# A hybrid decoder block on one core: gating and its loads on GpSimd, a staged gate table, and 512-wide products with u

## The chip, the cores and the metric

One core of a Trainium2 chip runs the whole program. TensorE (PE) multiplies, VectorE (DVE) and ScalarE (ACT) work on tiles and read PSUM, GpSimd (POOL) works on tiles in SBUF and issues indirect DMAs, SyncE (SP) issues the other DMAs. The metric is the device time of one execution in microseconds; a verdict rests on several runs.

## The reference

The block is `out = norm(h + PEER(norm(h)))` with `h = x + [attention, rwkv] @ W_out`, for 256 tokens of width 2048. The change lies in the last part, PEER: for each token and each of 8 heads two score lists of 128 keys are cut to their best 16, the 256 sums of pairs again to the best 16, and these name 16 of 128 x 128 = 16384 experts, with a softmax gate each.

```python
    hpre = jnp.einsum('cd,chkd->chk', xc, u[ec])
    act = jax.nn.gelu(hpre, approximate=False) * gc
    return jnp.einsum('chk,chkd->cd', act, v[ec])
```

All of it is float32, and the kernel keeps that precision by splitting operands into a high and a low part of type fp32r.

## The kernel before

It doesn't gather rows of u. It multiplies all 16384 rows of u with all 256 tokens, applies Gelu, multiplies with a dense table of gates (zero where an expert isn't chosen), and then goes through the rows of v in use only. The stages concerned, in time order:

*Hidden products* (`hidden`): 128 keys i2, each with the 128 experts (., i2). For a key `gemm` makes 16 steps of three 256-wide products: high weights with high tokens, high weights with low tokens, low weights with high tokens (lines 218 to 220). The weights come in halves of 512 KB on SP's queue (L197), split by ACT (L204) and DVE (L205). A Gelu (L1106) writes the key's 128x256 result into a tile A of eight keys.

*Beside them*, three generators get shares of a budget for every quarter of a key (`beside`, `run`): `both_choices` finds the experts, `tables` builds the table of gates, `scatter` writes rows away. Their `yield` values are costs against that budget; they set only where an instruction stands in its engine's order. Engines work in that order and wait by semaphores.

*The table* (`table`): for four columns (tokens) at a time DVE marks first and second key numbers (L931, L930), POOL scales the second mark by the gate's high part (L936), ACT by its low part (L938); TensorE multiplies the marks (L954), ACT and DVE bring the two halves of the result into a tile gc (L982, L983). Every 16 columns the tile goes to DRAM (`gate_d`), and POOL adds up (L969 to L976) which experts are in use. `places` then gives each expert a row in DRAM (`rows_d`).

*Rows* (`scatter`): for keys 0 to 125, DVE multiplies a key's Gelu results by its gates (L1074) and copies the expert's number beside them (L1088); POOL writes the 128 rows of 257 values to their places by an indirect DMA (L1089). The gates come back from `gate_d` in 16 loads of 1 MB (L1059, on SP's queue), one per eight keys.

*Products with v*: the last two keys skip the detour. Their gated results are split and multiplied with v as soon as the pool of the earlier stages is closed. For the others, blocks of 128 rows are read back once all scatters have landed, the rows of v are gathered (L1172, POOL), split and multiplied (L1159 to L1161), 108 blocks in all. A last norm follows.

The tiles A, gt (gates), at (rows), ob, gc, and later those of v all come from one pool of 16 buffers, so that a new one waits for the last reader of an old one.

Of the kernel before, what the change touches and what calls it, by code (L numbers as in the profile page):

```python
# [10 lines left out]
F32 = mybir.dt.float32  # L11
# [10 lines left out]
P = 128  # L22
# [132 lines left out]
def block_kernel(ctx: ExitStack, tc: tile.TileContext, x, cols, consts, w_lora, w_gate, w_rkv, w_qkv,  # L155
# [631 lines left out]
    nc.sync.dma_start(iota, consts[:, K_IO:K_IO + P])  # L787
    nh = mp.tile([P, KT, S], F32R, tag="mh", name="nh")
    nl = mp.tile([P, KT, S], F32R, tag="ml", name="nl")
    nhk, nlk = (lambda kt: nh[:, kt, 0:T]), (lambda kt: nl[:, kt, 0:T])  # L790
    sck = [chunked(f"sc{t}", 16, NKEY) for t in range(2)]

    def scores(b, ps):
# [5 lines left out]
        nc.vector.tensor_tensor(xn, hg(b), rstd2, op=ALU.mult)  # L799
        split(nh[:, b, :], nl[:, b, :], xn)  # L800
        yield
# [51 lines left out]
    def choose(t):  # L853
# [53 lines left out]
        yield 0.3  # L907
        nc.scalar.activation(tr, pt, AF.Copy)
        chosen[t] = tr
        yield 0.1  # L910

# [3 lines left out]
    def table(t):  # L915


        while t not in chosen:
            yield 0
        tr = chosen[t]  # L920
        b3 = [P, NB, P]
        col = lambda i, n: tr[:, i, n:n + NB].unsqueeze(2).to_broadcast(b3)
        row = iota.unsqueeze(1).to_broadcast(b3)
        made = {}

        def marks(n):
# [7 lines left out]
        def weighted(n):  # L934
            o1, o2, og = made[n]
            nc.gpsimd.tensor_tensor(og[:, :, 0, :], o2, col(2, n), op=ALU.mult)  # L936
            for i in range(NB):
                nc.scalar.activation(og[:, i, 1, :], o2[:, i, :], AF.Copy, scale=tr[:, 3, n + i:n + i + 1])  # L938

        marks(0)  # L940
        yield 0.1
        for q in range(8):
            gc = big(f"gc{q % 2}").rearrange("p (e t) -> p e t", t=16)
            late = []
            for n in range(q * 16, q * 16 + 16, NB):
                if n + NB < P:
                    marks(n + NB)
                weighted(n)
                yield 1.4
                o1, _, og = made.pop(n)  # L950
                for i in range(0, NB, 2):
                    ps = bank(("ch", "pw", "ch", "px")[(n // 2 + i // 2) % 4], [P, 2, 2, P])
                    for j in range(2):
                        nc.tensor.matmul(ps[:, j].rearrange("p a b -> p (a b)"), o1[:, i + j, :],  # L954
                                         og[:, i + j].rearrange("p a b -> p (a b)"), start=True, stop=True,
                                         skip_group_check=True)
                    late.append((ps, n + i - q * 16))
                    yield 0
                    if len(late) > 1:
                        ps_, k = late.pop(0)  # L960
                        evict(gc, ps_, k)
                        yield 0.45
            while late:
                evict(gc, *late.pop(0))
                yield 0.45
            nc.sync.dma_start(gate_d[:, t * 8 + q, :], gc.rearrange("p e t -> p (e t)"))

            w = big("mt")[:, 0:1024].rearrange("p (e t) -> p e t", t=8)
# [11 lines left out]
    def evict(gc, ps, k):  # L980
        g = gc[:, :, k:k + 2].rearrange("p e t -> p t e")
        nc.scalar.activation(g, ps[:, :, 1, :], AF.Copy)  # L982
        nc.vector.tensor_tensor(g, g, ps[:, :, 0, :], op=ALU.add)  # L983
# [124 lines left out]

# [181 lines left out]
```

## Time and profile before

| | |
|---|---|
| median of 3 runs | 2053.21 us (2050.47 to 2059.78) |
| profiled execution, its own time | 2050.37 us |
| its span, first to last instruction | 2048.6 us |
| TensorE, DVE, ACT, POOL busy | 94%, 72%, 51%, 32% of the span |
| mean granted clock of TensorE | 0.979 of full speed |

Busy shares are means over stages with different limits; what a stage waits for is read from its waits and windows. Times are in us from the span's start unless marked ns. A line number is the line of the kernel's source that issued the instruction; some lines are helpers with many callers.

### The profile page before, as it was taken

To read this page: it belongs to the slowest core of one execution; us is meant where nothing else is said; L and a number is where in the kernel's file an instruction comes from. 1 tells how busy PE (TensorE), PEld (TensorE's weight loads), DVE (VectorE), ACT (ScalarE), POOL (GpSimd) and SP (SyncE) were. 2 spreads that over 40 slices of the span, in tenths; PEclk is the share of its full clock that TensorE was granted. 3 is DMA by queue.
4 is the path that set the end of the run, shared out by engine and by line. 5 is a ranking of instruction groups with operands and counts; after the bars stand their busy time and mean duration, and the time that the engine had idled before them with its cause. 6 is when DMAs were issued, how large, how long until landed. Compare 5 with 4: busy or idle time off the path is not lost. (4 is left out here: it accounts for less than half of the span.)

```text
span 2048.6 us, 35160 instructions
## 1 busy us (share of the span) xinstructions
PE 1929.4 (94%) x13598; PEld 1810.1 (88%) x13598; DVE 1482.4 (72%) x2343; ACT 1054.0 (51%) x1636; POOL 654.5 (32%) x558
## 2 busy tenths in 40 slices
PE   7898999999999999998999999999993999999996
PEld 7798999999889999998999999999992888888885
DVE  6676878766557888999898887765553666666666
ACT  4544454454455444466676666534441655555554
POOL 7211221100000000135654545455547433333332
PEclk9999999999999999999999999999996999999998
DMA  8999322224665555455565655699898977888784
GB/s 251 259 255 243 100 78 93 88 84 154 211 218 188 185 178 176 164 172 185 197 217 188 215 182 180 229 306 297 286 296 273 368 275 278 299 286 299 280 292 149
DMA packets 163976, 444.14 MB, mean 217 GB/s; under 512 B 14368, under 2 KB 85024, under 8 KB 147168
## 3 DMA queue, kind: packets, MB, share of 16 engines
q1 hardware_dynamic: 140016, 306.02, 48.0%
q0 software_dynamic: 23792, 135.87, 18.1%
q8 instruction: 107, 1.75, 0.3%
q14 instruction: 61, 0.50, 0.1%
HBM read 380.07 MB, written 61.76 MB: 216 GB/s over the span
## 5 line engine op out<-in xcount | busy, mean ns | idle before, releaser
L204 ACT ACTIVATE whi<-raw 128x1024 fp32r<-128x1024 f32 (+1 forms) x408 | 431.2, 1057 | 501.9 <-PE ps_gm L219 220.9
L205 DVE TENSOR_TENSOR wlo<-raw,whi 128x1024 fp32r<-128x1024 f32 (+1 forms) x408 | 530.4, 1303 | 213.9 <-ACT whi L204 212.3
L220 PE MATMUL ps_gm<-nh,wlo 128*128 128x256 f32 x2048 | 585.6, 286 | 22.4 <-DVE wlo L205 21.7
L218 PE MATMUL ps_gm<-nh,whi 128*128 128x256 f32 x2048 | 583.0, 285 | 0.0
L219 PE MATMUL ps_gm<-nl,whi 128*128 128x256 f32 x2048 | 582.5, 284 | 0.0
L220 PEld LDWEIGHTS ps_gm<-nh,wlo 128*128 128x128 f32 x2048 | 396.1, 193 | 27.3 <-DVE wlo L205 26.9
L218 PEld LDWEIGHTS ps_gm<-nh,whi 128*128 128x128 f32 x2048 | 396.4, 194 | 0.0
L219 PEld LDWEIGHTS ps_gm<-nl,whi 128*128 128x128 f32 x2048 | 396.2, 193 | 0.0
L236 DVE TENSOR_TENSOR vlo<-vraw,vhi 128x2048 fp32r<-128x2048 f32 x108 | 247.8, 2296 | 146.3 <-ACT vhi L235 140.8
L235 ACT ACTIVATE vhi<-vraw 128x2048 fp32r<-128x2048 f32 x108 | 205.9, 1913 | 151.6 <-DVE vlo L236 144.4
L1172 POOL DMA_INDIRECT vraw<-in_v_dram,ag x108 | 145.0, 1343 | 285.0 <-PE ps_gm L1161 213.0
L218 PE MATMUL ps_gm<-xh,whi 128*128 128x256 f32 x640 | 192.8, 301 | 1.1 <-ACT whi L204 1.1
L220 PE MATMUL ps_gm<-xh,wlo 128*128 128x256 f32 x640 | 185.4, 290 | 1.3 <-DVE wlo L205 1.2
L219 PE MATMUL ps_gm<-xl,whi 128*128 128x256 f32 x640 | 186.0, 291 | 0.0
L1089 POOL DMA_INDIRECT rows_d<-at,place x126 | 143.3, 1137 | 117.4 <-DVE at L1088 66.4
L936 POOL TENSOR_TENSOR ob<-ob,pick 128x512 fp32r<-128x512 f32 x64 | 107.0, 1677 | 187.8 <-DVE ob L930 180.2
L220 PEld LDWEIGHTS ps_gm<-xh,wlo 128*128 128x128 f32 x640 | 123.1, 192 | 2.5 <-DVE wlo L205 1.9
L218 PEld LDWEIGHTS ps_gm<-xh,whi 128*128 128x128 f32 x640 | 123.3, 193 | 2.0 <-ACT whi L204 1.3
L219 PEld LDWEIGHTS ps_gm<-xl,whi 128*128 128x128 f32 x640 | 123.4, 193 | 0.7
L938 ACT ACTIVATE ob<-ob,pick 128x128 fp32r<-128x128 f32 x256 | 83.7, 389 | 61.4 <-DVE ob L930 61.3
L969 POOL TENSOR_TENSOR mt<-gc 128x1024 f32<-128x1024 f32 x16 | 55.0, 3434 | 166.3 <-DVE gc L983 166.3
L795 POOL DMA_DIRECT2D skb<-in_sk_dram x16 | 8.6, 539 | 250.7 <-ACT mh L235 167.7
(1528 smaller groups left out, 4027.2 us busy)
## 6 DMA issues: line engine op xcount, KB each, us to landing
raw<-in_u_dram SPq DMA_DIRECT2D x256, 512.0 KB, 4.1
raw<-in_w_rkv_dram SPq DMA_DIRECT2D x48, 512.0 KB, 6.9
raw<-in_w_qkv_dram SPq DMA_DIRECT2D x48, 512.0 KB, 3.3
rows_d<-zt SPq DMA_DIRECT2D x23, 1028.0 KB, 13.8
raw<-in_w_out_dram SPq DMA_DIRECT2D x32, 512.0 KB, 3.4
raw<-in_wq_dram SPq DMA_DIRECT2D x32, 512.0 KB, 3.4
gate_d<-gc SPq DMA_DIRECT2D x16, 1024.0 KB, 6.2
gt<-gate_d SPq DMA_DIRECT2D x16, 1024.0 KB, 9.0
```

The source lines that it names most:

```text
L204: nc.scalar.activation(hi[:, :n], raw[:, :n], AF.Copy)
L205: state["dve"] = nc.vector.tensor_tensor(lo[:, :n], raw[:, :n], hi[:, :n].bitcast(F32), op=ALU.subtract)
L218: nc.tensor.matmul(ps, a, xh(kt), start=first and k == 0, stop=False)
L219: nc.tensor.matmul(ps, a, xl(kt), start=False, stop=False)
L220: state["mm"] = nc.tensor.matmul(ps, b, xh(kt), start=False, stop=last and k == HK - 1)
L235: nc.scalar.activation(hi, src, AF.Copy)
L236: nc.vector.tensor_tensor(lo, src, hi.bitcast(F32), op=ALU.subtract)
L936: nc.gpsimd.tensor_tensor(og[:, :, 0, :], o2, col(2, n), op=ALU.mult)
L938: nc.scalar.activation(og[:, i, 1, :], o2[:, i, :], AF.Copy, scale=tr[:, 3, n + i:n + i + 1])
L969: nc.gpsimd.tensor_tensor(w, gc[:, :, 0:8], gc[:, :, 8:16], op=ALU.add)
L1089: s_ = nc.gpsimd.indirect_dma_start(out=rows_d, out_offset=bass.IndirectOffsetOnAxis(ap=place[:, i2:i2 + 1], axis=0), in_=at, in_offset=None)
L1172: nc.gpsimd.indirect_dma_start(out=raw, out_offset=None, in_=vf, in_offset=bass.IndirectOffsetOnAxis(ap=ag[:, T:ROW].bitcast(I32), axis=0))
```

## The change

Five things change together.

1. The tokens' high and low parts lie side by side, and `gemm_wide` multiplies the high weights with both in one 512-wide product, then the low weights with the high part in a 256-wide one. ACT copies the second half out, DVE adds the first, and the Gelu is issued a step into the next key.
2. The multiplication by the gates (`gated`) and the copy of the experts' numbers (now for seven keys at once) go to POOL, for the 126 scattered keys. The loads of gates go to POOL's queue.
3. The table is staged: marks, scaled marks and products of a group of columns stand in three successive turns. DVE makes the second mark and its gate in one operation per column; ACT scales that by the ratio of low and high part, worked out once in `choose`. POOL's multiplication L936 is gone.
4. The tile gc holds blocks of eight keys together, so that evictions write runs of eight.
5. `place` moves to a pool that stays open. The table's share of the budget is 0.43 for 0.45, a scatter's cost 1.5 for 2.35.

```diff
+    def gemm_wide(ps, xk):
+
...
+                nc.tensor.matmul(ps.rearrange("p z t -> p (z t)"), hi[:, k * P:(k + 1) * P],
+                                 x_.rearrange("p z t -> p (z t)"), start=i + k == 0, stop=False, skip_group_check=True)
+                state["mm"] = nc.tensor.matmul(ps[:, 0, :], lo[:, k * P:(k + 1) * P], x_[:, 0, :], start=False,
+                                               stop=i == 1 and k == HK - 1, skip_group_check=True)
...
-            o1, o2 = (ob[:, i * NB * P:(i + 1) * NB * P].rearrange("p (n k) -> p n k", n=NB) for i in range(2))
-            og = ob[:, 2 * NB * P:].rearrange("p (n z k) -> p n z k", n=NB, z=2)
-            nc.vector.tensor_tensor(o2, row, col(1, n), op=ALU.is_equal)
+            o1 = ob[:, 0:NB * P].rearrange("p (n k) -> p n k", n=NB)
+            og = ob[:, NB * P:3 * NB * P].rearrange("p (n z k) -> p n z k", n=NB, z=2)
             nc.vector.tensor_tensor(o1, row, col(0, n), op=ALU.is_equal)
-            made[n] = o1, o2.bitcast(F32), og
...
+        def weighted(n, i):
+            og = made[n][1]
+            c_ = lambda k: tr[:, k, n + i:n + i + 1]
+            nc.vector.tensor_scalar(og[:, i, 0, :], iota, c_(1), c_(2), op0=ALU.is_equal, op1=ALU.mult)
+            nc.scalar.activation(og[:, i, 1, :], og[:, i, 0, :].bitcast(F32), AF.Copy, scale=c_(3))
...
+        for n in range(0, P + 2 * NB, NB):
+            pairs = [half_in() for _ in range(1)] if late else []
+            if n < P:
+                marks(n)
+                yield 0.7
+            if pairs:
+                other_in(pairs.pop())
+                pairs.append(half_in())
+                yield 0.45
+            if NB <= n <= P:
+                for i in range(2):
+                    weighted(n - NB, i)
+                    yield 0.25
+            if pairs:
+                other_in(pairs.pop())
+                yield 0.45
+            if NB <= n <= P:
+                for i in range(2, NB):
+                    weighted(n - NB, i)
+                    yield 0.25
+            if 2 * NB <= n:
+                for i in range(0, NB, 2):
+                    product(n - 2 * NB, i)
+                made.pop(n - 2 * NB)
+                yield 0.02
+        while late:
+            other_in(half_in())
+            yield 0.45
         chosen[t, "table"] = True
...
-    place = sp.tile([P, P], I32, name="place")
+    place = cp.tile([P, P], I32, name="place")
...
-            nc.sync.dma_start(gts[g], gate_d[:, :, g * P:(g + 1) * P])
+            nc.gpsimd.dma_start(gts[g], gate_d[:, :, g * P:(g + 1) * P])
...
-    def gated(i2):
+    def gated(i2, eng=nc.gpsimd):
 
         if i2 % 7 == 0:
             rows[0] = big("at")
+            n = min(7, NKEY - i2)
+            eng.tensor_copy(rows[0][:, 0:n * ROW].rearrange("p (n c) -> p n c", c=ROW)[:, :, T].bitcast(I32),
+                                  eint[:, i2:i2 + n])
         g = gates_of(i2 // 8)
         if i2 % 8 == 1:
             gates_of(i2 // 8 + 1)
             gts.pop(i2 // 8 - 1, None)
         at = rows[0][:, i2 % 7 * ROW:(i2 % 7 + 1) * ROW]
         k = i2 % 8
-        nc.vector.tensor_tensor(at[:, 0:T].rearrange("p (q t) -> p q t", q=KT),
-                                As[i2 // 8][:, k, :].rearrange("p (q t) -> p q t", q=KT),
-                                g[:, :, 16 * k:16 * k + 16], op=ALU.mult)
+        eng.tensor_tensor(at[:, 0:T].rearrange("p (q t) -> p q t", q=KT),
+                          As[i2 // 8][:, k, :].rearrange("p (q t) -> p q t", q=KT),
+                          g.rearrange("p q (t b) -> p q t b", b=8)[:, :, :, k], op=ALU.mult)
...
-            nc.vector.tensor_copy(at[:, T:ROW].bitcast(I32), eint[:, i2:i2 + 1])
...
-            yield 2.35
-
+            yield 1.5
...
-            ps = bank("gm")
-            yield from gemm(ps[:, :T], P, nhk, nlk)
-            state["gelu"] = nc.scalar.activation(As[-1][:, i2 % 8, 0:T], ps[:, :T], AF.Gelu)
-            hid["n"] = i2 + 1
+            ps = bank("gm", [P, 2, S])
+            wide = gemm_wide(ps, nk)
+            next(wide)
+            if summed:
+                gelu()
+            yield
+            yield from wide
+            part = small("part")
+            nc.scalar.activation(part, ps[:, 1, :], AF.Copy)
+            nc.vector.tensor_tensor(part, part, ps[:, 0, :], op=ALU.add)
+            summed.append((part, As[-1][:, i2 % 8, :], i2))
+        gelu()
...
-    beside = [[both_choices(), 0.55, 0.0], [tables(), 0.45, 0.0], [scatter(), 1.0, 0.0]]
+    beside = [[both_choices(), 0.55, 0.0], [tables(), 0.43, 0.0], [scatter(), 1.0, 0.0]]
...
-            ah, al_ = halves_of(gated(i2)[:, 0:T])
+            ah, al_ = halves_of(gated(i2, nc.vector)[:, 0:T])
```

POOL's order, where the scatters begin, before: `at` is a tile of seven rows, and what stands in brackets is whose semaphores the instruction waits for (DMASW0 to 7 are those of POOL's own DMAs, used in turn).

```order
L973 TENSOR_TENSOR mt<-mt 128x128 [waits Pool_49]
L974 TENSOR_TENSOR act_8194<-act_8194,mt 128x128 [waits Pool_49]
L1089 DMA rows_d<-at,place 39936x257 [waits DVE_49]
L1089 DMA rows_d<-at,place 39936x257 x5
L1089 DMA rows_d<-at,place 39936x257 [waits DMASW6_49]
L1089 DMA rows_d<-at,place 39936x257 [waits DMASW7_49,DVE_49]
L1089 DMA rows_d<-at,place 39936x257 [waits DMASW0_49,DVE_49]
L1089 DMA rows_d<-at,place 39936x257 [waits DMASW1_49,DVE_49]
```

And of the change, some way into the same stretch (`A` a tile of eight keys, `gt` its gates):

```order
L1122 TENSOR_TENSOR at<-A_9660,gt_14731 128x256
L1122 TENSOR_TENSOR at<-A_10268,gt_14863 128x256 [waits DMASW5_49]
L1136 DMA rows_d<-at,place 39936x257 [waits DMASW4_49,Pool_49]
L1136 DMA rows_d<-at,place 39936x257 [waits Pool_49]
L1104 DMA gt_14981<-gate_d 128x16x128 [waits DMASW6_49]
L1122 TENSOR_TENSOR at<-A_10268,gt_14863 128x256 x2
L1136 DMA rows_d<-at,place 39936x257 [waits DMASW7_49,Pool_49]
L1136 DMA rows_d<-at,place 39936x257 [waits DMASW0_49,Pool_49]
L1114 COPY at<-eint 128x7
L1122 TENSOR_TENSOR at<-A_10268,gt_14863 128x256
L1122 TENSOR_TENSOR at<-A_10268,gt_14863 128x256 [waits Pool_49]
L1136 DMA rows_d<-at,place 39936x257 [waits DMASW1_49,Pool_49]
```

Before, POOL has nothing but scatters there, each waiting for DVE. Now a multiplication stands for each, mostly in pairs ahead of a pair of scatters, with the loads and copies between them, and the waits are for POOL itself.

DVE's order in the table stage, before (L205 is the split of weights, L983 the eviction):

```order
L930 TENSOR_TENSOR ob<-iota,pick 128x512
L931 TENSOR_TENSOR ob<-iota,pick 128x512
L205 TENSOR_TENSOR wlo<-raw,whi 128x1024 x2
L983 TENSOR_TENSOR gc_12201<-gc_12201,ps_ch 128x2x128
L930 TENSOR_TENSOR ob<-iota,pick 128x512
L931 TENSOR_TENSOR ob<-iota,pick 128x512
L930 TENSOR_TENSOR ob<-iota,pick 128x512
L205 TENSOR_TENSOR wlo<-raw,whi 128x1024
L983 TENSOR_TENSOR gc_12201<-gc_12201,ps_pw 128x2x128
L931 TENSOR_TENSOR ob<-iota,pick 128x512
```

And of the change (L954 the scaled marks, L1167 the addition that follows a wide product, L996 the eviction):

```order
L205 TENSOR_TENSOR wlo<-raw,whi 128x1024
L954 TENSOR_SCALAR ob<-iota,pick 128x128 x4
L948 TENSOR_TENSOR ob<-iota,pick 128x512
L205 TENSOR_TENSOR wlo<-raw,whi 128x1024
L1167 TENSOR_TENSOR part<-part,ps_gm 128x256
L996 TENSOR_TENSOR gc_11420<-gc_11420,ps_ch 128x2x16x8
L996 TENSOR_TENSOR gc_11420<-gc_11420,ps_pw 128x2x16x8
L954 TENSOR_SCALAR ob<-iota,pick 128x128 x3
L205 TENSOR_TENSOR wlo<-raw,whi 128x1024
L954 TENSOR_SCALAR ob<-iota,pick 128x128 x5
L205 TENSOR_TENSOR wlo<-raw,whi 128x1024
```

One of two 512-wide marks is gone, four 128-wide ones stand in its place, and each key adds a 256-wide addition.

ACT's order of the change, where the Gelu (L1151) of key 104 opens a new tile A:

```order
L204 ACTIVATE whi<-raw 128x1024 [waits DMAHW1_49,PE_49,Activation_49]
L204 ACTIVATE whi<-raw 128x1024 [waits DMAHW2_49,PE_49,Activation_49]
L1166 ACTIVATE part<-ps_gm 128x256 [waits PE_49]
L1151 ACTIVATE A_15175<-part 128x256 [waits DVE_49,Pool_49]
L204 ACTIVATE whi<-raw 128x1024 [waits DMAHW3_49,PE_49,Activation_49]
L204 ACTIVATE whi<-raw 128x1024 [waits DMAHW4_49,PE_49,Activation_49]
L1166 ACTIVATE part<-ps_gm 128x256 [waits PE_49]
```

This first Gelu of a tile waits for POOL, since the buffer was one that POOL's multiplications read; behind it stand the splits of the next weights.

## Rows read from the trace of the kernel before

**Rows 1.** Windows of the span by stage: engine busy (x instructions), clock, DMA share, GB/s.
```profile
733.00:850.00 117.00, 117.00 (x978) 117.00 (x977) 101.53 (x255) 53.59 (x67) 0.00 (x0) 1.00 0.55 180
850.00:950.00 100.00, 88.77 (x698) 87.96 (x697) 97.19 (x135) 63.12 (x127) 42.59 (x23) 0.95 0.50 164
950.00:1310.00 360.00, 343.65 (x2821) 340.61 (x2820) 311.31 (x314) 240.70 (x467) 191.14 (x115) 1.00 0.61 198
1336.90:1553.40 216.50, 209.03 (x1721) 206.92 (x1720) 131.41 (x300) 85.37 (x109) 121.54 (x105) 1.00 0.93 303
1553.40:1581.50 28.10, 0.00 (x0) 0.00 (x0) 5.31 (x15) 1.06 (x1) 21.70 (x22) 0.50 0.63 225
1581.50:1599.00 17.50, 14.88 (x57) 11.82 (x58) 5.46 (x7) 7.27 (x10) 6.49 (x9) 0.83 0.90 326
1599.00:2010.00 411.00, 411.00 (x1814) 340.24 (x1814) 268.89 (x202) 227.41 (x202) 137.29 (x101) 1.00 0.82 295
```

**Rows 2.** Waits, 1540 to 1600 us: who waited for whom, total, times, longest.
```profile
PE ps_mm L1159 <- ACT ah L235: 34.6, 1, 34.6
ACT ah L235 <- DMA rows_d<-at,place: 22.0, 1, 22.0
```

**Rows 3.** Timeline: start, length, engine, what, idle before; POOL and PE near 1590 us.
```profile
1580.58 0.96 POOL L1089 DMA_INDIRECT rows_d<-at,place  x1 [0.30 <-issue]
1583.91 0.77 PE L1159 MATMUL ps_mm<-whi,ah 128*128 128x512 f32 x1 [34.64 <-ACT ah L235]
1596.50 0.40 PE L1159 MATMUL ps_mm<-vhi,ah 128*128 128x512 f32 x1
```

**Rows 4.** The scatters of L1089: busy and idle before, then shortest, median and longest.
```profile
L1089 POOL DMA_INDIRECT rows_d<-at,place x126 | 143.3, 1137 | 117.4 <-DVE at L1088 66.4 <-issue 21.6 <-DVE place L1044 16.0
L1089 POOL DMA_INDIRECT rows_d<-at,place x126: 963/972/2292, 1336.9 to 1580.6; - x126
```

**Rows 5.** Timeline of POOL: the two scatters that waited longest.
```profile
1414.11 0.97 POOL L1089 DMA_INDIRECT rows_d<-at,place  x1 [17.16 <-DVE at L1088]
1509.12 0.97 POOL L1089 DMA_INDIRECT rows_d<-at,place  x1 [18.35 <-DVE at L1088]
```

**Rows 6.** POOL's 128x256 operations: one alone, first stage by lines, tables by lines.
```profile
292.58 0.60 POOL L360 TENSOR_TENSOR df<-ext 128x256 f32<-128x256 f32 x1 [11.84 <-DVE y L531]
L360 POOL TENSOR_TENSOR df<-ext 128x256 f32<-128x256 f32 x26 | 20.9, 804 | 143.7 <-DVE ext L358 131.7 <-DVE y L531 11.8
L971 POOL TENSOR_TENSOR mt<-mt 128x256 f32<-128x256 f32 x16 | 17.7, 1104 | 1.3
```

**Rows 7.** Direct DMAs on POOL by line: 96, 128 and 256 runs.
```profile
L370 POOL DMA_DIRECT2D l<-in_a_dram x8: 512/513/570, 4.0 to 238.6; - x8
L795 POOL DMA_DIRECT2D skb<-in_sk_dram x16: 535/535/577, 548.3 to 721.8; - x16
L539 POOL DMA_DIRECT2D gg<-in_g_dram x8: 714/747/757, 34.4 to 379.9; - x8
```

**Rows 8.** Lines of DVE and POOL, 950 to 1310 us: busy, mean ns, idle before.
```profile
L205 DVE TENSOR_TENSOR wlo<-raw,whi 128x1024 fp32r<-128x1024 f32 x110 | 160.3, 1464 | 36.7 <-ACT whi L204 36.5
L931 DVE TENSOR_TENSOR ob<-iota,pick 128x512 fp32r<-128x512 f32 x51 | 63.8, 1251 | 0.0
L983 DVE TENSOR_TENSOR gc<-gc,ps_ch 128x256 f32<-128x256 f32 x52 | 32.6, 626 | 6.8 <-ACT gc L982 5.9
L936 POOL TENSOR_TENSOR ob<-ob,pick 128x512 fp32r<-128x512 f32 x51 | 84.6, 1664 | 32.1 <-DVE ob L930 32.1
```

**Rows 9.** One line each: shortest, median, longest; then key 91's Gelu in the timeline.
```profile
L1004 DVE TENSOR_SCALAR wk<-act x2: 219/222/226, 1320.9 to 1321.0; 128x128 f32<-128x128 f32 x2
L358 DVE TENSOR_TENSOR ext<-ps_gm,rstd x24: 381/425/427, 53.8 to 305.1; 128x256 f32<-128x256 f32 x24
L1106 ACT ACTIVATE A<-ps_gm x128: 354/366/387, 739.3 to 1553.0; 128x256 f32<-128x256 f32 x128
1336.93 0.37 ACT L1106 ACTIVATE A<-ps_gm 128x256 f32<-128x256 f32 x1
```

More of the change, by code (lines that the diff above doesn't have):

```diff
@@ L232, in gemm @@
             yield from gemm_half(ps, width, xh, xl, range(i * HK, (i + 1) * HK), i == 0, i == 1)
+    def gemm_wide(ps, xk):
+        for i in range(2):
+            hi, lo = half()
+            for k in range(HK):
+                x_ = xk(i * HK + k)
+                nc.tensor.matmul(ps.rearrange("p z t -> p (z t)"), hi[:, k * P:(k + 1) * P],
+                                 x_.rearrange("p z t -> p (z t)"), start=i + k == 0, stop=False, skip_group_check=True)
+                state["mm"] = nc.tensor.matmul(ps[:, 0, :], lo[:, k * P:(k + 1) * P], x_[:, 0, :], start=False,
+                                               stop=i == 1 and k == HK - 1, skip_group_check=True)
+                if k % 4 == 3:
+                    yield
     def split(hi, lo, src):
@@ L787, in block_kernel @@
     nc.sync.dma_start(iota, consts[:, K_IO:K_IO + P])
-    nh = mp.tile([P, KT, S], F32R, tag="mh", name="nh")
-    nl = mp.tile([P, KT, S], F32R, tag="ml", name="nl")
-    nhk, nlk = (lambda kt: nh[:, kt, 0:T]), (lambda kt: nl[:, kt, 0:T])
+    nx = [mp.tile([P, HK, 2, S], F32R, tag=tag, name="nx") for tag in ("mh", "ml")]
+    nk = lambda kt: nx[kt // HK][:, kt % HK]
     sck = [chunked(f"sc{t}", 16, NKEY) for t in range(2)]
@@ L799, in scores @@
         nc.vector.tensor_tensor(xn, hg(b), rstd2, op=ALU.mult)
-        split(nh[:, b, :], nl[:, b, :], xn)
+        split(nk(b)[:, 0, :], nk(b)[:, 1, :], xn)
         yield
@@ L908, in choose @@
         nc.scalar.activation(tr, pt, AF.Copy)
+        rh = small("rh")[:, 0:P]
+        nc.vector.tensor_scalar(rh, tr[:, 2, :], 1e-36, None, op0=ALU.max)
+        nc.vector.reciprocal(rh, rh)
+        yield 0.6
+        nc.vector.tensor_tensor(tr[:, 3, :], tr[:, 3, :], rh, op=ALU.mult)
         chosen[t] = tr
-        yield 0.1
+        yield 0.3
     NB = 4
@@ L934, in weighted @@
[L934 to L968, printed above, removed]
@@ new lines, in marks, with sums @@
+            made[n] = o1, og
+        def weighted(n, i):
[3 more added lines that the diff above has]
+            nc.scalar.activation(og[:, i, 1, :], og[:, i, 0, :].bitcast(F32), AF.Copy, scale=c_(3))
+        def sums(q, gc):
+            nc.sync.dma_start(gate_d[:, t * 8 + q, :], gc.rearrange("p a t b -> p (a t b)"))
+            w = big("mt")[:, 0:1024].rearrange("p (a t b) -> p a t b", t=8, b=8)
@@ L980, in evict @@
[L980 to L983, printed above, removed]
-    place = sp.tile([P, P], I32, name="place")
+                nc.gpsimd.tensor_tensor(w[:, :, 0], w[:, :, 0], w[:, :, 1], op=ALU.add)
+                nc.gpsimd.tensor_tensor(a_, a_, w[:, :, 0], op=ALU.add)
+            else:
+                nc.gpsimd.tensor_tensor(a_, w[:, :, 0], w[:, :, 1], op=ALU.add)
@@ new lines, in table, with product, half_in @@
+        gcs, late = {}, []
+        def product(n, i):
+            o1, og = made[n]
+            ps = bank(("ch", "pw", "ch", "px")[(n // 2 + i // 2) % 4], [P, 2, 2, P])
+            for j in range(2):
+                nc.tensor.matmul(ps[:, j].rearrange("p a b -> p (a b)"), o1[:, i + j, :],
+                                 og[:, i + j].rearrange("p a b -> p (a b)"), start=True, stop=True,
+                                 skip_group_check=True)
+            late.append((ps, n + i))
+        def half_in():
+            ps, n = late[0]
+            q = n // 16
+            if q not in gcs:
+                gcs[q] = big(f"gc{q % 2}").rearrange("p (a t b) -> p a t b", t=16, b=8)
+            k = n % 16
+            g = gcs[q][:, :, k:k + 2].rearrange("p a t b -> p t a b")
+            nc.scalar.activation(g, ps[:, :, 1, :].rearrange("p t (a b) -> p t a b", b=8), AF.Copy)
+            return g
@@ new lines, in other_in @@
+        def other_in(g):
+            ps, n = late.pop(0)
+            nc.vector.tensor_tensor(g, g, ps[:, :, 0, :].rearrange("p t (a b) -> p t a b", b=8), op=ALU.add)
+            if n % 16 == 14:
+                sums(n // 16, gcs.pop(n // 16))
+        for n in range(0, P + 2 * NB, NB):
[8 more added lines that the diff above has]
+            if NB <= n <= P:
+                for i in range(2):
+                    weighted(n - NB, i)
[12 more added lines that the diff above has]
+                yield 0.02
@@ L1096, in scatter, with gelu @@
             done.append(s_)
-            yield 2.35
+            yield 1.5
+    summed = []
+    def gelu():
+        part, dst, i2 = summed.pop()
+        state["gelu"] = nc.scalar.activation(dst, part, AF.Gelu)
+        hid["n"] = i2 + 1
     def hidden():
```

6 lines of the change are left out of this document (2 added, 4 removed).

## The prediction

> **What bounds the kernel now.** I read the page's slices first. TensorE is at 9 tenths nearly everywhere, with one hole about three quarters through. The table of windows shows its size: from 1553.4 to 1581.5 us TensorE does nothing, and after 1599 it never waits [rows 1]. So there are two questions: what ends the hole, and what sets its start.
>
> The waits name the end. The first product with v stood 34.6 us behind ACT's split of a row, and ACT 22.0 us behind a DMA into rows_d, one of the scatters of L1089 [rows 2]. GpSimd (POOL) issues the last scatter at 1580.58 and is done at 1581.54; TensorE starts at 1583.9 with the two keys that are kept back, and the first gathered product comes at 1596.5 [rows 3]. Everything behind the last scatter (2048.6 - 1581.5 = 467.1 us) is untouched by the change. **The time is the end of the last scatter plus 467 us, plus the 1.8 us that the profiled time of 2050.37 us has over its span.** The end of the hidden products, 1553.4, leads the scatters by 28 us and sets nothing.
>
> Hence the stretch to take apart is POOL's, from the first scatter at 1336.89 to 1581.54: 244.7 us for 126 scatters. 143.3 us are busy; the idle time before them is 117.4, of which 16.0 lie before the first, so 101.4 us are gaps inside [rows 4]. Between two scatters that follow one another stands 0.30 us [rows 3], 125 times, 37.5 us. The remaining 64 us are waits for rows that VectorE (DVE) had not gated yet; the largest are 17.2 and 18.4 us [rows 5], when the gate table's next load stood on SP's queue. The same queue loads u.
>
> **The change, part by part.** *Gating on POOL.* The 126 multiplications leave DVE, and the 64 us of waits with them. They come back as POOL's own work, in the same queue as the scatters: the order shows pairs of multiplications and pairs of scatters, with nothing else to do the work. No such multiplication is in the trace, but POOL does other 128x256 ones: 0.60 us undisturbed, 0.80 on average in the first stage, 1.10 in the tables beside a DVE that is 86% busy [rows 6, 1]. In the scatter stretch DVE was 61% busy and will lose the gating, but keeps two splits of 1.2 us per key. I take 0.80, from the row with the middle load: 101 us, with 76 and 139 as ends.
> [...]
>
> *Loads of the gate table on POOL.* 14 of the 16 stand between the first scatter and the last. Each has 2048 runs of 512 bytes. Issuing a direct DMA on POOL took 0.513 us with 96 runs, 0.535 with 128 and 0.747 with 256 [rows 7]. The slope between the first two gives 1.9 us for 2048 runs, that between the last two 3.7; no growth at all gives 0.54. I take 1.9, the middle one: 27 us, ends 8 and 52.
> [...]
>
> *Copies of the row numbers.* 18 of 7 columns instead of 126 of one on DVE. Nothing in the trace is like them on POOL; between nothing and the 0.60 us of a 256-wide operation, 0 to 11 us; I take 0.2 us each, 4 us.
>
> *Scatters themselves* stay: 143 us, or 122 if each took the median of 0.972 [rows 4]. The 0.30 us before each stays (37 us); if the multiplication in front of a pair hides one of the two, 19.
>
> So the stretch becomes 143 + 37 + 101 + 27 + 4 = 312 us against 244.7: **+68 us**. It is no longer paced by DVE; what is late next is POOL itself.
>
> *The start of the stretch.* Scatters begin when the places are known, in both kernels beside key 91 of the hidden products (their Gelu stood at 1336.93 [rows 9]). Three things move it.
> (a) The wide product. A 256-wide product takes 117/978 = 119.6 ns, a 512-wide one 411/1814 = 226.6 [rows 1]. Three of 256 become one of 512 and one of 256: 346 for 359 ns, 12.6 ns times 2048 = 26 us over all 128 keys, 18 by key 91, but only where TensorE is the bound.
> (b) What it adds: per key one copy on ACT, like the Gelu's 0.37 us, and one addition on DVE, 0.42 like other 256-wide ones from PSUM [rows 9].
> (c) The table, between 950 and 1310. DVE loses the mark of L931 (64 us), gains four scaled marks of 128 columns per four columns, 0.22 us each like L1004 (204 of them, 45 us), and the additions of (b), 54 keys, 23 us: +4 us. Its 103 evictions of L983 take 0.63 us, 0.2 more than a 256-wide read of PSUM elsewhere [rows 8, 9]; they write every sixteenth element now and runs of eight after, so I count 0.42: -21 us, and as much on ACT, which evicts the other half. POOL loses L936, 85 of its 191 busy us, and with it part of what lengthens DVE's splits (1.46 us on average here, about 1.22 undisturbed, 110 times, 27 us): at 85/191 of that -12 us [rows 8, 1]. DVE, 311 of 360 us busy, ends near 282; ACT stays at 240; TensorE goes from 344 to 332 [rows 1]. TensorE is then the bound, and 28 us could be won; since all three wait for one another in order, I take three quarters: -21 us. Between 850 and 950 DVE is 97% busy, and the additions weigh 14 times 0.42 = 6 against 3 of lighter evictions: +3. Before 850, where TensorE never waits, 10 keys give -2 until the choices fill DVE. Sum -20; ends 0 and -35.
>
> Keys 92 to 127 then run beside POOL. The order shows that the Gelu of keys 96, 104, 112 and 120 waits for POOL, since its tile is one that POOL reads. A POOL that needs 2.48 us a row stalls ACT there, and TensorE behind it. This costs nothing in the sum, because the last scatter ends later still. `place` moves out of the pool that is closed before the products with v, so the 12.6 us of the two kept keys (1583.9 to 1596.5) can run before the last scatter; the gathered rows still come some 15 us after it [rows 3], so nothing is won.
>
> **Sum:** 2050.4 + 68 - 20 = **2098 us**, where the median of the runs, 2053.2, stands 2.8 us above the profiled execution.
>
> **Rivals.** *POOL keeps up* (faster). The multiplications find DVE's pauses and take 0.60, one of two gaps is hidden, loads cost 0.54, scatters 0.972: 122 + 19 + 76 + 8 = 225 us, with the start 20 earlier about 2010; with one of the four at my middle value some 2025. For it: DVE has half its time free there. Against it: four terms have to be at their low ends together, and in the stretch as it is scatters take 1.14 on average. It decides at (244.7 + 20)/126 = 2.10 us of POOL per row, everything in.
> *A draw.* POOL's added work just eats the 64 us of waits and the earlier start: 2050.
> *The loads come late* (slower still). On POOL's queue each DMA waits for the landing of the eighth before it, and the loads of 1 MB now share the scatters' queue. If a load lands 4 us after its first use, 14 times, 56 us are added: 2154. Against it: each is issued some seven rows, 16 us, ahead.
> *The wide product gives nothing.* True wherever the end is set by POOL; then it is in my number already.
>
> **How the numbers follow.** POOL as the bound 0.60, POOL keeps up 0.20, the draw 0.10, late loads 0.10. A measurement tells 0.5%, 10 us, from no change: faster 0.20, same 0.10, slower 0.70. All low ends with the best start would be 1996 (2050 - 20 - 35), all high ends without one 2188 (143 + 37 + 139 + 52 + 11 = 382, 138 more); eight times in ten I expect 2025 to 2145, and, if POOL is the bound, 2065 to 2135.
>
> **What would show it.** POOL 9 tenths busy or more from the first scatter to the last, with no long wait for DVE; its multiplication near 0.80, its loads near 1.9, about 2.48 us a row; the first scatter near 1317; ACT's Gelu waiting for POOL in the last 24 keys; a hole of TensorE before the gathered products that is wider than 28 us. I am wrong if the last scatter ends before 1571: then POOL's rows cost under 2.10 us, or the table won more than 35 us.

## The result and the profile after

The changed kernel takes **2121.52 us** (median of 4 runs, 2118.63 to 2123.94) against 2055.03 us before: ratio 1.0327, 95% interval [1.0308, 1.0346]. The forecast was 2098, with 2025 to 2145 as its range. The span of the profiled execution is 2119.2 us against 2048.6, 70.6 us more.

The forecast cut the time at the first and the last scatter. So cut, with the same cuts in the kernel before:

| us | before | changed | difference | forecast |
|---|---|---|---|---|
| up to the first scatter | 1336.9 | 1324.3 | -12.6 | -20 |
| first scatter to the end of the last | 244.7 | 318.7 | +74.0 | +68 |
| from there to the end | 467.1 | 476.2 | +9.1 | 0 |
| sum | 2048.6 | 2119.2 | +70.6 | +48 |

The windows of the changed kernel, with the columns of [rows 1]:

```profile
850.00:950.00 100.00, 86.97 (x460) 71.71 (x460) 98.51 (x211) 60.46 (x126) 12.70 (x9) 0.97 0.49 153
950.00:1312.00 362.00, 353.63 (x2054) 307.88 (x2053) 310.71 (x566) 245.17 (x547) 102.06 (x70) 1.00 0.67 213
1324.00:1643.00 319.00, 216.87 (x1166) 183.88 (x1164) 138.77 (x115) 98.29 (x148) 286.31 (x278) 0.86 0.65 218
```

In the stretch of scatters POOL (fifth engine) is busy 286 of 319 us; before it was 143 of 245. TensorE has 217 us of work there, against 209 us in the shorter stretch before, so it is no longer the engine that works almost without a pause. POOL by lines, from the first scatter on (busy and mean ns, then idle time before them):

```profile
L1136 POOL DMA_INDIRECT rows_d<-at,place x126 | 152.1, 1207 | 31.3 <-issue 19.2 <-POOL at L1122 11.8 <-DVE wlo L205 0.3
L1122 POOL TENSOR_TENSOR at<-A,gt 128x256 f32<-128x256 f32 x120 | 114.2, 971 | 1.4
L1104 POOL DMA_DIRECT2D gt<-gate_d x14 | 17.0, 1213 | 0.0
L1114 POOL COPY at<-eint 128x7 int32<-128x7 int32 x17 | 4.5, 268 | 0.0
```

152.1 + 31.3 + 114.2 + 1.4 + 17.0 + 4.5 make 320.5 us, within 2 us of the stretch (instructions that follow one another overlap: the four busy times sum to 287.8 us, the window has 286.3). No row waits for DVE any more, against 66.4 us behind L1088 in [rows 4], and the scatters' idle time is only the 0.3 us ahead of an issue. One round of the timeline shows the pattern, two multiplications and two scatters, and then ACT's Gelu of key 104, which waits for POOL:

```profile
1397.45 1.83 POOL L1122 TENSOR_TENSOR at<-A,gt 128x256 f32<-128x256 f32 x2
1399.44 1.81 POOL L1136 DMA_INDIRECT rows_d<-at,place  x1 [0.17 <-POOL at L1122]
1401.56 0.97 POOL L1136 DMA_INDIRECT rows_d<-at,place  x1 [0.30 <-issue]
1402.56 1.79 POOL L1122 TENSOR_TENSOR at<-A,gt 128x256 f32<-128x256 f32 x2
...
1421.49 0.42 ACT L1151 ACTIVATE A<-part 128x256 f32<-128x256 f32 x1 [23.32 <-POOL at L1122]
```

Up to that Gelu the hidden results (by the start of ACT's copy or, before, of its Gelu) came out some 14 us ahead of those before; key 105's is 6 us late, and the last one 15. The waits from 1550 to 1700 us, who for whom, total, times, longest, answer to [rows 2]:

```profile
PE ps_mm L1221 <- ACT ah L248: 63.6, 1, 63.6
DVE at L1122 <- DMA gt<-gate_d: 48.5, 1, 48.5
```

TensorE's hole is 63.6 us instead of 34.6. It ends with the two kept keys, whose gates DVE got from a load that stood in POOL's queue until 1610.60. It doesn't set the time: in e2 below, where that load is on SP's queue, the hole is 30.7 us and the stretch behind the last scatter as long as here (476.9).

### The profile page after: what moved, and what is told of

It is laid out like the page before. It is cut to its first block, busy times and chain, and to the rows that moved or that the text cites. A ratio compares the mean times of both kernels' runs of the same rounds, so it can differ in the third digit from the quotient of the medians.

```text
span 2119.2 us, 31321 instructions
## 1 busy us (share of the span) xinstructions
PE 1924.9 (91%) x11550; PEld 1701.6 (80%) x11550; DVE 1474.6 (70%) x2418; ACT 1066.9 (50%) x1764; POOL 677.2 (32%) x654
## 5 line engine op out<-in xcount | busy, mean ns | idle before, releaser
L240 PE MATMUL ps_gm<-nx,whi 128*128 128x512 f32 x2048 | 732.2, 400 | 30.7 <-ACT whi L204 22.2
L205 DVE TENSOR_TENSOR wlo<-raw,whi 128x1024 fp32r<-128x1024 f32 (+1 forms) x408 | 550.4, 1353 | 247.1 <-ACT whi L204 244.3
L242 PE MATMUL ps_gm<-nx,wlo 128*128 128x256 f32 x2048 | 581.7, 284 | 19.9 <-DVE wlo L205 19.8
L240 PEld LDWEIGHTS ps_gm<-nx,whi 128*128 128x128 f32 x2048 | 388.3, 190 | 121.7 <-ACT whi L204 22.9
L242 PEld LDWEIGHTS ps_gm<-nx,wlo 128*128 128x128 f32 x2048 | 391.0, 191 | 29.7 <-DVE wlo L205 29.3
L248 ACT ACTIVATE vhi<-vraw 128x2048 fp32r<-128x2048 f32 x108 | 205.9, 1913 | 161.1 <-DVE vlo L249 146.8
L961 POOL TENSOR_TENSOR mt<-gc 128x1024 f32<-128x1024 f32 x16 | 42.9, 2682 | 460.0 <-DVE gc L996 417.7
L1136 POOL DMA_INDIRECT rows_d<-at,place x126 | 152.1, 1207 | 31.3 <-issue 19.2
L1151 ACT ACTIVATE A<-part 128x256 f32<-128x256 f32 x128 | 53.1, 415 | 212.4 <-DVE part L1167 167.2
L1122 POOL TENSOR_TENSOR at<-A,gt 128x256 f32<-128x256 f32 x126 | 122.0, 988 | 6.8 <-DMA gt<-gate_d 5.3
L955 ACT ACTIVATE ob<-ob,pick 128x128 fp32r<-128x128 f32 x256 | 87.8, 395 | 34.5 <-DVE ob L954 30.7
L954 DVE TENSOR_SCALAR ob<-iota,pick 128x128 fp32r<-128x128 f32 x256 | 82.6, 370 | 0.0
```

What stands on the lines that cost most here:

```text
L205: state["dve"] = nc.vector.tensor_tensor(lo[:, :n], raw[:, :n], hi[:, :n].bitcast(F32), op=ALU.subtract)
L240: nc.tensor.matmul(ps.rearrange("p z t -> p (z t)"), hi[:, k * P:(k + 1) * P], x_.rearrange("p z t -> p (z t)"), start=i + k == 0, stop=Fa ...
L242: state["mm"] = nc.tensor.matmul(ps[:, 0, :], lo[:, k * P:(k + 1) * P], x_[:, 0, :], start=False, stop=i == 1 and k == HK - 1, skip_group_ ...
L248: nc.scalar.activation(hi, src, AF.Copy)
L1122: eng.tensor_tensor(at[:, 0:T].rearrange("p (q t) -> p q t", q=KT), As[i2 // 8][:, k, :].rearrange("p (q t) -> p q t", q=KT), g.rearrange( ...
L1136: s_ = nc.gpsimd.indirect_dma_start(out=rows_d, out_offset=bass.IndirectOffsetOnAxis(ap=place[:, i2:i2 + 1], axis=0), in_=at, in_offset=None)
```

## The experiments

A table first, since most verdicts are read from the three cuts. "First key" is the start of the copy of key 0's hidden result (of its Gelu in e4, e10 and the kernel before), the next column the time from there; all times in us, spans of the profiled executions. Chips differ in the part ahead of it (739.3 us in the kernel before, 749.2 in e4, whose edit stands behind it), and the cuts of one run are compared with those of another chip's in places; the ratios are each to the kernel before on the same chip. e6 and e9 are judged by their ratios alone. Differences of under 2% are read from the intervals.

| | first key | to first scatter | scatters | rest | ratio to before, interval |
|---|---|---|---|---|---|
| before | 739.3 | 597.6 | 244.7 | 467.1 | 1 |
| changed | 742.1 | 582.2 | 318.7 | 476.2 | 1.0327 [1.0308, 1.0346] |
| e1 | 749.9 | 581.2 | 299.4 | 477.2 | 1.0186 [1.0168, 1.0205] |
| e2 | 751.0 | 582.4 | 300.3 | 476.9 | 1.0249 [1.0232, 1.0266] |
| e3 | 748.1 | 582.6 | 253.6 | 475.0 | 1.0013 [0.9988, 1.0038] |
| e4 | 749.2 | 607.1 | 298.3 | 468.8 | 1.0308 [1.0291, 1.0325] |
| e5 | 739.4 | 613.5 | 243.8 | 468.2 | 1.0078 [1.0048, 1.0108] |
| e6 | | | | | 0.9990 [0.9974, 1.0006] |
| e7 | 741.7 | 601.2 | 214.0 | 477.3 | 0.9915 [0.9885, 0.9945] |
| e8 | 738.2 | 603.1 | 239.9 | 470.9 | 0.9999 [0.9981, 1.0016] |
| e9 | | | | | 0.9920 [0.9875, 0.9965] |
| e10 | 753.1 | 577.8 | 242.8 | 480.5 | 0.9762 [0.9697, 0.9826] |
| e11 | 749.5 | 584.4 | 423.7 | 475.0 | 1.0582 [1.0515, 1.0649] |
| e12 | 751.6 | 585.1 | 236.8 | 476.8 | 0.9719 [0.9664, 0.9773] |

The last four (e9 to e12) ran on a chip where the kernel before took 2104 us (2111 beside e12) instead of 2054 to 2065, so their ratios hold more than their edits. Why is open; the traces of e9, e10 and e12 show single waits of up to 12, 15 and 9 us of ACT's splits of u there, with a releaser that the profile doesn't name.

**e1, gating back on DVE, gate loads still on POOL.**

```diff
-    def gated(i2, eng=nc.gpsimd):
+    def gated(i2, eng=nc.vector):
```

> The changed kernel with the multiplications by the gates and the copies of row numbers back on DVE; the loads of gates stay in POOL's queue, all else as changed. If POOL is the bound (my theory): per scatter 1.2 us busy and 0.3 before it, and 14 loads of 1.2 us, 204 us in all from the first scatter near 1324, so about 1528; the last Gelu of a scattered key comes later than that, near 1535, so the last scatter ends at 1540 to 1550 and the time is 2010 to 2025. If the products with u lost the time (additions on DVE, copies on ACT): the time stays at 2105 to 2125. If the loads in POOL's queue lost it: over 2090.

Measured 2104.78 us, ratio 1.0186: my number was missed by over 80 us, and the time is one that the rival "the loads in POOL's queue" gives (the products with u, the other rival, are kept in e3, which loses nothing). POOL's queue should have needed only some 177 us (126 scatters of 0.97 with 0.30 ahead of each, 17 us of loads), and still the scatters took 299. POOL's scatters by lines, the waits from 1310 to 1700 us, and POOL around one load:

```profile
L1136 POOL DMA_INDIRECT rows_d<-at,place x126 | 193.9, 1539 | 91.4 <-DVE at L1122 56.6 <-issue 26.5 <-DMA rows_d<-at,place 3.0
```

```profile
DVE at L1122 <- DMA gt<-gate_d: 82.9, 7, 19.5
PE ps_gm L240 <- DVE part L1167: 67.3, 13, 19.3
```

```profile
1372.81 1.42 POOL L1136 DMA_INDIRECT rows_d<-at,place  x1 [0.30 <-issue]
1374.22 1.20 POOL L1104 DMA_DIRECT2D gt<-gate_d  x1
1381.35 6.51 POOL L1136 DMA_INDIRECT rows_d<-at,place  x1 [5.92 <-DVE at L1122]
```

The load for DVE's next rows stands behind POOL's earlier scatters, and lands 8.2 us (median) after its issue. DVE, which works in order, waits 82.9 us for such loads, with the splits and additions that TensorE needs behind them. The loads aren't the whole of the excess: the scatters themselves were busy for 193.9 us instead of 122, which also happens in e3, without these loads (see the last section). What the loads cost is read from e3, which differs from e1 in their queue alone: 45.8 us of scatters (299.4 against 253.6). Where POOL itself gates, the same loads cost 18.4 (e2), about the 17.0 us of their issue.

**e2, the changed kernel with gate loads on SP; e3, with gating on DVE as well.**

```diff
-            nc.gpsimd.dma_start(gts[g], gate_d[:, :, g * P:(g + 1) * P])
+            nc.sync.dma_start(gts[g], gate_d[:, :, g * P:(g + 1) * P])
```

> The changed kernel with only the loads of gates back in SP's queue; POOL still multiplies. POOL as the bound: its queue loses 17 us of loads but may wait for loads that stand behind those of u, as DVE did before; 2100 to 2125. If the loads in POOL's queue lost the time: 2050 to 2060.

> The changed kernel with gating on DVE and loads of gates in SP's queue, so that only the wide product, the staged table and the new layout of the gates are left of the change. POOL as the bound: the scatters take the 245 us that they took before, from 1324, and the time is 2035 to 2045, faster than before. If the rest of the change loses the time: over 2060.

e2: 2114.56 us, within what POOL as the bound gives, and far from the 2050 to 2060 of the rival. The scatters are 18.4 us shorter than in the changed kernel, the 17.0 us of the loads. e3: 2065.93 us, no difference from before. So between e3 and e2, with nothing moved but the gating and the copies of the row numbers, lie 46.7 us of scatters. But e3 isn't the 2035 to 2045 that I expected: the rest of the change wins nothing either.

**e4, the kernel before with the multiplications alone on POOL.**

```diff
-        nc.vector.tensor_tensor(at[:, 0:T].rearrange("p (q t) -> p q t", q=KT),
+        nc.gpsimd.tensor_tensor(at[:, 0:T].rearrange("p (q t) -> p q t", q=KT),
```

> The kernel before with nothing but the multiplications by the gates moved to POOL (row numbers still copied by DVE one column at a time, loads in SP's queue). POOL as the bound: 150 us of scatters, 37 of gaps and 115 of multiplications, 302 us and waits for loads of up to 40, from 1337; the time is 2110 to 2150. If the loss came from another part: 2050 to 2060.

2127.97 us, ratio 1.0308: this one edit loses nearly as much as the whole change, which also holds gains and losses that cancel (e3). POOL by lines in its stretch of 298 us:

```profile
L1089 POOL DMA_INDIRECT rows_d<-at,place x126 | 154.2, 1224 | 42.9 <-issue 18.9 <-DVE at L1088 13.1 <-POOL at L1074 10.8
L1074 POOL TENSOR_TENSOR at<-A,gt 128x256 f32<-128x256 f32 x120 | 103.8, 885 | 1.5
```

**e5, the kernel before with the 512-wide product alone; e6, with the staged table and its layout alone.** The edits are the part of the diff in `gemm_wide`, `nx` and `hidden`, and that in `table` and `gated` with DVE and SP kept.

> The kernel before with the 512-wide product with u alone (copy on ACT, addition on DVE, Gelu a step later). If the end is the last scatter plus a fixed rest, it is worth only what it brings the first scatter forward, at most 18 us, less the 15 us of additions on DVE beside the scatters: ratio to before 0.992 to 1.000. If the added copy and addition sit in the way of the products: over 1.005.

> The kernel before with the staged table and the new layout of the gates, and the seven-column copies; gating on DVE, loads of gates in SP's queue, cost of a scatter 2.35 as before. The table wins up to 20 us ahead of the first scatter; the multiplications read every eighth gate and take 0.66 us instead of 0.42, 30 us more of DVE beside the scatters. If that eats the gain: 0.995 to 1.010. If the layout costs nothing: 0.988 to 0.993.

e5: 2069.88 us, 0.8% slower, not faster. Its scatters last as long as before (243.8) and begin 15.9 us later. Key 24 is 5.4 us ahead, key 33 is 8.8 late and key 91 14.7. So the wide product wins while TensorE is the bound, and the loss comes while choices and table fill DVE, first of all from 850 to 950 us. Windows with the columns of [rows 1], of the kernel before and then of e5:

```profile
745.00:830.00 85.00, 85.00 (x711) 85.00 (x710) 69.59 (x156) 39.06 (x49) 0.00 (x0) 1.00 0.56 183
```

```profile
745.00:830.00 85.00, 85.00 (x492) 75.05 (x491) 75.41 (x200) 44.75 (x69) 0.00 (x0) 0.95 0.61 185
850.00:950.00 100.00, 80.91 (x433) 68.35 (x434) 100.00 (x171) 63.24 (x129) 35.34 (x22) 0.89 0.46 148
```

From 745 to 830 us a step of three products takes 359 ns before (711 products) and a step of two 346 ns here (492). From 850 to 950 DVE has no pause, and the new addition, 0.414 us per key, stands in its order; over nine keys that is 4 us and not the 14 that are lost between keys 24 and 33, so how the rest comes about isn't shown. The lower granted clock of this execution, 0.95 in the first window, isn't it: the changed kernel has the same 492 products from 745 to 830 us at 1.00. e6: no difference, as expected if the layout eats the table's gain.

**e7, as e3 with the old layout of the gates; e8, as e7 with a scatter's cost of 2.35.**

```diff
-                          g.rearrange("p q (t b) -> p q t b", b=8)[:, :, :, k], op=ALU.mult)
+                          g[:, :, 16 * k:16 * k + 16], op=ALU.mult)
```

> As e3 (gating on DVE, loads of gates in SP's queue), but the gates laid out as before, so that a multiplication reads runs of 16 again; the evictions of the table write every sixteenth element again. If the layout is what eats the gain of the table and the wide product: the multiplication goes back to 0.42 us, and the ratio is 0.983 to 0.992. If not: 0.997 to 1.005, as e3.

> As e7 with a scatter's cost of 2.35 instead of 1.5, so that DVE does not get up to four multiplications in a row. If bunched multiplications hold up POOL's scatters (in e3 scatters lasted up to 8 us while DVE worked without a pause): 5 to 15 us below e7 and scatters of under 2.5 us. If not: within 4 us of e7.

e7: 2037.11 us, 0.9915: the layout ate the gain. It brings the first scatter forward by 18.6 us (582.6 against 601.2) and costs 39.6 us of scatters (253.6 against 214.0), in which POOL's scatters are busy for 212.7 us against 146.8 (last section). DVE's multiplications, shortest, median and longest ns, in e3 and in e7:

```profile
L1122 DVE TENSOR_TENSOR at<-A,gt x128: 609/678/796, 1323.6 to 1580.3; 128x256 f32<-128x256 f32 x128
```

```profile
L1121 DVE TENSOR_TENSOR at<-A,gt x128: 410/421/464, 1336.3 to 1566.5; 128x256 f32<-128x256 f32 x128
```

e8 fell the other way from what I had thought: a cost of 2.35 loses 17.6 us to e7; the scatters take 25.9 more (239.9), and the rest gives 6.4 back. POOL waits 57.8 us for DVE's rows there and 37.4 in e7. DVE's rows have to stand early in its order; several in a row do no harm there, where they read their gates in runs (scatters busy for 146.8 us in e7, 150.4 in e8).

**e9, the kernel before with a cost of 1.5; e10, e6 with that cost and the gates laid out in pairs of keys.**

```diff
-            yield 2.35
+            yield 1.5
```

```diff
-                gcs[q] = big(f"gc{q % 2}").rearrange("p (a t b) -> p a t b", t=16, b=8)
+                gcs[q] = big(f"gc{q % 2}").rearrange("p (a t b) -> p a t b", t=16, b=2)
```

> The kernel before with one number changed, a scatter's cost of 1.5 instead of 2.35: DVE's multiplications stand earlier in its order. If the 64 us of waits for rows in the kernel before come from that order and not from gate loads that land late: the stretch of scatters shrinks until key 125's Gelu sets its end, 20 us or more, ratio 0.983 to 0.992. If late loads make the waits: 0.997 to 1.003.

> The kernel before with the staged table and a cost of 1.5, products with u as before, gating on DVE, loads in SP's queue, and a third layout of the gates: keys in pairs, so that evictions write runs of four and a multiplication reads every second gate. If short runs are enough for the evictions (0.42 us) and every second gate reads near full speed (0.42 to 0.50): the first scatter some 20 us earlier and no loss behind it, ratio 0.972 to 0.983. If the read costs 0.66 as with every eighth: 0.99 or more.

e9: 2096.38 us, 0.992 with an interval from 0.9875 to 0.9965: it wins something on that chip, at the small end of what the order of DVE's rows was to give. e10: the pairs cost neither side anything. Evictions and multiplications, in ns as above:

```profile
L984 DVE TENSOR_TENSOR gc<-gc,ps_ch x64: 398/418/446, 878.6 to 1304.8; 128x256 f32<-128x256 f32 x64
...
L1110 DVE TENSOR_TENSOR at<-A,gt x128: 414/421/452, 1322.8 to 1584.1; 128x256 f32<-128x256 f32 x128
```

**e11, the changed kernel with each of POOL's multiplications done twice.**

```diff
+        if eng is nc.gpsimd:
+            eng.tensor_tensor(at[:, 0:T].rearrange("p (q t) -> p q t", q=KT),
```

> The changed kernel with each of POOL's 126 multiplications done twice in a row. If POOL's queue is the bound in the stretch of scatters, each costs its whole 0.97 us: 115 to 122 us more than the changed kernel, ratio to before 1.085 to 1.095. If POOL has slack and the loss comes from loads or the products with u: under 1.06.

2236.09 us; the ratio of 1.058 is below what I gave, as that chip's kernel before is slower, so the trace decides: the scatters take 423.7 us, 105.0 more than in the changed kernel (I gave 115 to 122, at 0.97 us each), for these second multiplications (L1126):

```profile
L1126 POOL TENSOR_TENSOR at<-A,gt 128x256 f32<-128x256 f32 x123 | 109.5, 905 | 1.0
```

All but a few per cent of what is put into POOL's queue comes out at the end. POOL has no slack in the changed kernel.

**e12, e3 with pairs of keys.**

> As e3 (wide product with u, staged table, gating on DVE, loads of gates in SP's queue, a scatter's cost of 1.5), with the gates laid out in pairs of keys as in e10. There evictions took 0.40 to 0.42 us and multiplications 0.42. If the two costs of the layout are what stood between e3 and e7: the table of e3 (first scatter near 580 us after the first hidden row) and the stretch of scatters of e7 (213 us) together, ratio 0.978 to 0.987. If the stretch only waits for what the table wins: 0.990 to 0.995, as e7.

2044.17 us against 2111.01 before, beside it on that chip. It beats the kernel before there; its scatters (236.8) didn't come down to e7's 214.0. Whether it beats e7, which took 2037.11 us on another chip, isn't shown.

## Why the prediction was right, point by point

*POOL is the bound.* Right, and shown in three ways: put on POOL, the multiplications cost 46.7 us of scatters (e3 to e2) and 53.6 (before to e4); done twice, 105 more (e11). The figures "about 2.48 us a row" and "312 us" came out as 318.7/126 = 2.53 and 318.7.

*The terms of the sum.* Scatters 152 for 143, gaps 31 for 37, copies 4.5 for 4. Two were mis-sized against one another. The multiplication was "0.80, from the row with the middle load" and took 0.97: e4, with runs of 16 gates, has 0.885 (shortest 0.712); with every eighth gate 0.971 (shortest 0.841). The layout, which I priced for the evictions only, adds 0.13 to the shortest; in the means it is 0.09 from e4 to the changed kernel and 0.03 from e4 to e2 (0.913), so its share of the miss stays open between a sixth and a half; the rest stands in e4 already, without the layout. The loads were "1.9 us for 2048 runs" and took 1.21: the slope from 96 to 128 runs carried too far. e2 prices them at 18 us, where I had 27. That "312 us" came so near is luck in part: the multiplications (+13) and the scatters (+9) were too low, the loads (-10) and the gaps (-6) too high. The rival of the late loads didn't happen: POOL waited for a load once, for 5.3 us, ahead of the first scatter; in e1, where DVE gates, loads in that queue do come late. "POOL keeps up" and the draw fell with the terms: of the four that had to be low, loads and gaps came out under my middle values, none at its low end.

*The start, -20.* Measured -12.6. By stages the forecast held better than that: key 33 is level with the kernel before (forecast +1 by 950 us) and keys 33 to 91 win 18.7 us (forecast -21), counted from the first key. What I hadn't counted is 2.8 us ahead of the first key, and 3.3 at the seam: key 91's copy is at 1320.98, but POOL had six multiplications to do, and a load to issue, ahead of the first scatter at 1324.26. The working behind the -21 failed, though. "TensorE is then the bound" rested on DVE "near 282", and DVE was busy for 311 of 362 us; that 18.7 came out all the same is luck. By parts, (a) the wide product alone loses 15.9 us (e5): its price was right, 346 ns a step for 359 between 745 and 830 us, but while choices and table fill DVE it isn't TensorE that it has to relieve. The evictions of (c) were right: L996 takes 0.412 us instead of 0.626, and the first scatter comes 18.6 us earlier (e7 to e3) for the -21 of evictions. The rest of the table, with the lower cost of a scatter, gives 12.3 us (e5 to e7). Together that is -15.0, against -15.4 from the first key. The rows that answer to [rows 8], from 950 to 1312 us:

```profile
L205 DVE TENSOR_TENSOR wlo<-raw,whi 128x1024 fp32r<-128x1024 f32 x117 | 159.7, 1366 | 34.4 <-ACT whi L204 34.3
L954 DVE TENSOR_SCALAR ob<-iota,pick 128x128 fp32r<-128x128 f32 x210 | 64.9, 363 | 0.0
L1167 DVE TENSOR_TENSOR part<-part,ps_gm 128x256 f32<-128x256 f32 x57 | 23.4, 411 | 1.2 <-ACT part L1166 1.2
L996 DVE TENSOR_TENSOR gc<-gc,ps_ch 128x256 f32<-128x256 f32 x54 | 22.2, 412 | 3.0 <-ACT gc L991 3.0
```

The scaled mark was the other miss: 0.363 us where "0.22 us each like L1004" was counted, 0.14 times 210 = 30 us of DVE, which is what lies between 282 and 311. The splits fell from 1.464 to 1.366, 11.5 us over 117 of them, as the -12 said.

*The rest, "untouched by the change".* 9.1 us more, and here the step fell that put nothing at it. The first gathered product comes 19.9 us after the last scatter's end instead of 15.0: the first rows of v reach ACT's split 11.3 us after POOL's issue instead of 6.3 (the four rows below, before and then of the change; why they land later isn't shown). Another 4.2 us go behind it: up to 1670.5 the products run at a granted clock of 0.50, one every 0.43 us, and then at 0.99, one every 0.23 us. The 24 us ahead of them hold 6 us of TensorE's work; whether that set the clock isn't shown. Of the kept keys' 48 products 36 were done by 1639.1; the last twelve came from 1650.2 on, since their weights' split stands on ACT behind the split of the first row read back, which waits for the scatters.

```profile
1588.13 0.98 POOL L1172 DMA_INDIRECT vraw<-in_v_dram,ag  x1 [6.00 <-ACT ah L235]
1594.43 1.92 ACT L235 ACTIVATE vhi<-vraw 128x2048 fp32r<-128x2048 f32 x1 [2.98 <-DMA vraw<-in_v_dram,ag]
```

```profile
1649.59 1.00 POOL L1234 DMA_INDIRECT vraw<-in_v_dram,ag  x1 [6.00 <-DMA ag<-rows_d]
1660.93 1.91 ACT L248 ACTIVATE vhi<-vraw 128x2048 fp32r<-128x2048 f32 x1 [10.50 <-DMA vraw<-in_v_dram,ag]
```

Windows of the change, as above:

```profile
1638.80:1662.90 24.10, 6.09 (x15) 3.76 (x13) 2.01 (x4) 3.58 (x4) 9.57 (x11) 0.67 0.79 289
1662.90:1670.50 7.60, 6.07 (x13) 4.41 (x14) 6.79 (x4) 5.18 (x4) 0.94 (x1) 0.50 1.03 423
1670.50:1690.00 19.50, 19.50 (x87) 16.16 (x86) 14.24 (x11) 12.11 (x12) 7.11 (x5) 0.99 0.80 291
```

In [rows 3] the first gathered product took 0.40 at once, right behind the kept keys. e4 and e5, in which `place` stays where it was, have 468.8 and 468.2 us of rest; e1, e2, e3, e7 and e8, in which it moves, have 470.9 to 477.3. That fits, but no run moved `place` alone, and on the last chip, where the kernel before is slower as a whole, the rest doesn't tell them apart. "So nothing is won" was true; that something is lost I hadn't seen.

*The 64 us of waits in the kernel before.* I put them down to gate loads stuck in SP's queue. That reading was wrong for the larger part. DVE's waits for such loads before, from 1337 to 1582 us (total, times, longest):

```profile
DVE at L1074 <- DMA gt<-gate_d: 25.4, 11, 4.2
```

None of them falls into the two long waits of [rows 5], 17.2 and 18.4 us: there DVE went through splits of u that stand ahead of the rows in its order. e7 against e8 shows that this order, set by the cost of 2.35, makes a part of the waits: with 1.5 POOL waits 20 us less.

## What to carry to other kernels

Before moving work to an idle engine, count that engine's queue in the stretch that sets the end, not over the span: POOL was busy a third of the time, but in its stretch it had 64 us of waits for some 136 us of new work (multiplications, loads and copies). An engine's loads shouldn't stand in a queue behind instructions that wait for that same engine (e1: DVE waited 82.9 us for such loads, and the scatters took 45.8 us more than in e3). And a layout has two sides: price the reader with the writer.

## What the runs showed of the hardware that was not expected

What a stride in an operand cost depended on its size. A 256-wide DVE operation took 0.63 us where it wrote every sixteenth element (evictions before), 0.68 where it read every eighth (e3), and 0.42 in runs (e7); where it read every second element (e10) it took 0.42 as well. On POOL the median went from 0.739 in runs of 16 (e4) to 0.922 with every eighth (the changed kernel). Why is not shown.

Scatters on POOL, 0.97 us in the median before ([rows 4]), lasted up to 8.2 us in e3, 212.7 us in all against e7's 146.8, while DVE worked without a gap. POOL, then DVE beside it:

```profile
1382.05 8.15 POOL L1136 DMA_INDIRECT rows_d<-at,place  x1 [0.30 <-issue]
```

```profile
1382.23 1.85 DVE L1122 TENSOR_TENSOR at<-A,gt 128x256 f32<-128x256 f32 x3
1383.97 1.25 DVE L205 TENSOR_TENSOR wlo<-raw,whi 128x1024 fp32r<-128x1024 f32 x1
1385.11 1.31 DVE L1122 TENSOR_TENSOR at<-A,gt 128x256 f32<-128x256 f32 x2
```

In e7, with DVE as dense but its gates read in runs, such a stretch leaves scatters of 1.2 to 1.8 us:

```profile
1376.29 1.24 POOL L1135 DMA_INDIRECT rows_d<-at,place  x1 [1.74 <-DVE at L1121]
1377.83 1.39 POOL L1135 DMA_INDIRECT rows_d<-at,place  x1 [0.30 <-issue]
1379.53 1.45 POOL L1135 DMA_INDIRECT rows_d<-at,place  x1 [0.30 <-DVE at L1113]
1381.28 1.83 POOL L1135 DMA_INDIRECT rows_d<-at,place  x1 [0.30 <-issue]
```

e1, which has the strided reads too, shows 193.9 us of scatters; e12, which is e3 with pairs, 152.1. So in e1 and e3, where DVE reads every eighth gate, POOL's indirect DMAs are held up; by what way is not shown. The direct DMAs in e1's POOL queue show nothing of the kind: all 16 loads of gates took 1.16 to 1.21 us to issue, though whether DVE read its gates beside one of them isn't shown. The other direction shows too: with POOL multiplying (the changed kernel), DVE's splits averaged 1.695 us in the stretch, against 1.223 before, with the longest at 3.4; in e4, where POOL reads its gates in runs, they averaged 1.386.
